# Mixer output projections: low parts of the first three weight tiles made by VectorE, and the first mixer's third tile prepared earlier

## The chip, the cores and the metric

The kernel runs on one core of a Trainium2 chip. The metric is the device time of one execution in microseconds (us); lower is better. Five engines work on one core side by side, each through its own list of instructions in a fixed order: TensorE (PE; its weight loads are listed as PEld), VectorE (DVE), ScalarE (ACT), GpSimd (POOL) and SyncE (SP), which here only issues DMAs. An instruction waits for semaphores that others raise, and while it waits everything behind it on its engine waits too.

## The reference, cut to what matters

Two groups of tokens, 512 and 256, pass through the same two layers. Each layer is a half SwiGLU block, a mixer, and another half SwiGLU block, with a residual sum around each. The change touches only the last step of the two mixers, the product with `w_out`:

```
def mixer_ab(h, ...):                       # layer 0
    z = h @ w_in
    a_out = u * vmix                        # spatial gating, 512 columns
    b_out = window_gqa(q, k, v, sink)       # windowed attention, 512 columns
    return jnp.concatenate([a_out, b_out], axis=-1) @ w_out

def mixer_c(h, w_qkv, rpb, w_out):          # layer 1
    qkv = h @ w_qkv
    o = neighbourhood_attn(q, k, v, rpb)
    return o @ w_out

x = x + mixer(rmsnorm(x, mix_n), ...)
```

All data is float32. `w_out` is 1024 x 1024 in both layers.

## The kernel before, in words

**Tiling.** Activations lie transposed: 8 tiles of 128 features by 768 tokens. A product is cut into output tiles of 128 features (m = 0 to 7) by two halves of 384 tokens (h = 0, 1), and sums over 8 input tiles k. A float32 product is made from three passes on rounded parts: each operand is a high part plus a low part, and `mm3` issues weight-high by data-high, weight-high by data-low, weight-low by data-high. The high part is a ScalarE copy into the rounded type (line 122 for weights, 208 for data), the low part a subtraction source minus high part (line 123 for weights, 209 for data). `wsplit` makes both parts of a weight tile of 128x512; its subtraction runs on GpSimd unless it is given an engine.

**Names in the trace.** `raw` is a weight tile as loaded, `whi` and `wlo` its parts; `o` is the mixer's result before the projection, `oh` and `ol` its parts; `eh` and `el` are parts of two of those tiles made early in the first mixer; `th`, `tl`, `p`, `st` and `tb` belong to the attention; `xold` is the residual, read back from DRAM in the first mixer; `ps_mm` and `ps_aux` are PSUM tiles.

**The projection, `mixer_out`.** Six of the eight input tiles are ready before attention ends; their products come first, for the output tiles m = 0 to 5 (`first`). The last two input tiles follow when attention has ended (`second`). The weights of output tile m come from `rows(m)`. For an even m it loads the weights of two output tiles: one tile of 512 KB with the first four input rows, and one of 256 KB with rows 4 and 5. The second of these is split at once, by ScalarE and VectorE (`unit`); I call it the pair's end tile. Then `rows` splits the four rows of its own m by `wsplit`; I call that m's row tile. So an even m makes two splits and an odd m one.

The first mixer (layer 0) takes the input tiles in the order 4, 5, 0, 1, 2, 3, the second mixer (layer 1) in the order 0, 1, 2, 3, 4, 5. So the first product of an output tile reads the end tile in the first mixer, and the row tile in the second. In the first mixer the output tiles 0 and 1 are begun early, with the two input tiles that are ready first; the splits of the remaining input tiles (`parts`) come between. In the second mixer `ready` splits all six input tiles, both halves, 12 pairs of `oh` and `ol`, before the first product.

**What sets the order.** On TensorE the order is that of the program. Beside the projection, generators that are stepped by a running estimate of TensorE's time put attention in between (`tick`). On all other engines a scheduler orders the instructions as the program is built, by its own estimate of when each could start; that order is fixed when the kernel runs. Loaded weights and `xold` share four buffers (`rawp`), `whi` and `wlo` have five each.

Of the kernel before, what the change touches and what calls it, by code (L numbers as in the profile page):

```python
# [16 lines left out]
P = 128  # L17
# [38 lines left out]
class Trunk:  # L56
# [914 lines left out]
    def mixer_out(self, name, ot, chain, cols=False, begun=None):  # L971

        nc = self.nc
        early, late = (4, 5, 0, 1, 2, 3) if cols else range(KD - 2), (KD - 2, KD - 1)
        oh, ol = ([self.gp.tile([P, T], F32R, tag=f"x{n}{k}", name=f"o{n}{k}") for k in range(KD)] for n in "hl")
        src = (oh, ol)
        self.x = [None] * KD
        old = {}  # L980

        def parts(ks, h):
            c0, c1 = HALVES[h]
            for k in ks:
                self.split(oh[k][:, c0:c1], ol[k][:, c0:c1], ot[k][:, c0:c1])

        def ready(ks, done=()):
            for h in (0, 1):
                parts([k for k in ks if (k, h) not in done], h)
            for k in ks:  # L990
                self.x[k] = self.xp.tile([P, T], F32, tag=f"x{k}", name=f"x{k}")
                if not cols:
                    nc.sync.dma_start(self.x[k], self.xd[k])

        def put(m, h, ps):

            c0, c1 = HALVES[h]
            x = self.x[m]
            if not cols:
                nc.vector.tensor_tensor(out=x[:, c0:c1], in0=ps[:, :H], in1=x[:, c0:c1], op=ALU.add)  # L1000
                return
            if h == 0:
                old[m] = self.rawp.tile([P, T], F32, tag="raw", name="xold")
                nc.sync.dma_start(old[m], self.xd[m])
            for a, b in ((H, TA), (TA, T)) if h else ((0, H),):
                out, rows = self.by_column(x, slice(0, P), a, b)
                nc.vector.tensor_tensor(out=out, in0=rows(ps[:, a - c0 : b - c0]), in1=rows(old[m][:, a:b]), op=ALU.add)

        def plus(m, h, ps):
            x = self.x[m][:, HALVES[h][0] : HALVES[h][1]]  # L1010
            nc.vector.tensor_tensor(out=x, in0=ps[:, :H], in1=x, op=ALU.add)
            self.final(m, *HALVES[h])

        loaded = {}

        def rows(m):
            if m % 2 == 0:
                loaded[4] = self.raw(name, 0, 4, m * P, 2 * P)
                loaded[2] = self.unit(name, 4, 2, m * P, 2 * P)
            c = m % 2 * P  # L1020
            hi, lo = self.wsplit(loaded[4][:, :, c : c + P])
            return [(hi[:, k, :], lo[:, k, :]) for k in range(4)] + [tuple(t[:, c : c + P] for t in k) for k in loaded[2]]

        def first(m, h, w):
            put(m, h, self.proj(w, src, HALVES[h], ks=early))

        def second(m, h):
            st = [tuple(t[:, k, m % 2 * P : m % 2 * P + P] for t in ends[m // 2]) for k in (0, 1)]
            plus(m, h, self.proj([None] * 6 + st, src, HALVES[h], ks=late))

        def end(i):
            if i % 2 == 0:
                loaded["end"] = self.raw(name, KD - 2, 2, i * 2 * P, 4 * P)
            c = i % 2 * 2 * P
            ends.append(self.wsplit(loaded["end"][:, :, c : c + 2 * P]))

        alone = ()
        if begun:
            alone = (0, 1)
            w = [rows(m) for m in alone]  # L1040
            done = [self.proj(w[m], begun, (0, H), ks=early[:2], last=False) for m in alone]
            rest = early[2:]
            with self.tc.high_priority(), self.tc.issue_after(self.exps[-1]):
                parts(rest, 0)
            for m in alone:
                ps = self.proj(w[m], src, HALVES[0], ps=done[m], ks=rest, first=False)
                if m == 0:
                    parts(early, 1)
                    parts(early[:2], 0)
                    ready(early, [(k, h) for k in early for h in (0, 1)])  # L1050
                put(m, 0, ps)
            for m in alone:
                first(m, 1, w[m])
        else:
            ready(early)
        for m in range(len(alone), KD - 2):
            w = rows(m)
            for h in (0, 1):
                first(m, h, w)
        self.drain(chain)  # L1060
        with self.tc.issue_after(self.exps[-1]):
            self.silu()
        ready(late)
        self.ffn_open(self.close("mp"))
        self.ffn_tiles()
        self.mixed = True
        self.norm_begin(self.following)
        ends = []
        w = rows(6)
        end(0)  # L1070
        first(6, 0, w)
        end(1)
        for m in (0, 1):
            second(m, 0)
        first(6, 1, w)
        for m in (2, 3):
            second(m, 0)
        w = rows(7)
        end(2)
        for h in (0, 1):  # L1080
            first(7, h, w)
        end(3)
        for m in range(4, KD):
            second(m, 0)
        self.half_done(0)
        for m in range(KD):
            second(m, 1)
        self.close("xg")
        self.fw = self.open("work", self.other(self.guards["comb"][1]))
        self.half_done(1)  # L1090
# [732 lines left out]
```

## Time and profile before

| | |
|---|---|
| median of 3 runs | 2592.6 us (2591.68 to 2593.29) |
| the profiled execution | 2593.14 us, of which 2591.4 us from first to last instruction |
| TensorE matmul busy | 2552.9 us, 99% |
| VectorE busy | 2234.0 us, 86% |
| ScalarE busy | 1366.5 us, 53% |
| GpSimd busy | 159.4 us, 6% |
| granted TensorE clock, mean | 0.996 |
| weight subtractions on GpSimd | 36, 1349 ns each |
| the same on VectorE | 468 from `raw`, 695 ns each |

The profile names each group of instructions by line, engine, operation and tiles. "Idle before" is the time that the engine stood still just ahead of an instruction, with the instruction that ended the wait behind the arrow. In a timeline the columns are start, duration, engine, line and operation, tiles, shapes and count; neighbours of one kind are merged, and the duration is then that of the group. In a table by windows, PEclk is the share of the full clock that TensorE was granted. The first mixer's projection lies at about 682 to 780 us of the span, the second's at about 2006 to 2100 us.

### The profile page before, as it was taken

How to read it: one execution, taken by the hardware profiler on the slowest of the kernel's cores; microseconds unless marked ns; L12 is line 12 of the kernel's file. 1: busy time of each engine (PE TensorE's matmuls, PEld its weight loads, DVE VectorE, ACT ScalarE, POOL GpSimd, SP SyncE). 2: the span in 40 equal slices, each digit the busy share in tenths (PEclk: the TensorE clock that was granted, in tenths of full speed). 3: DMA queues.
4: the chain of work that ended last, by engine and by line, in shares of the span. 5: the costliest groups of instructions: out<-in, count | busy, mean ns of one | idle time of the engine just before them, and what ended most of it. 6: DMA issues, size and time to landing. Idle time of an engine off the chain costs nothing.

```text
span 2591.4 us, 41313 instructions
## 1 busy us (share of the span) xinstructions
PE 2552.9 (99%) x15114; PEld 2488.1 (96%) x15114; DVE 2234.0 (86%) x4659; ACT 1366.5 (53%) x2869; POOL 159.4 (6%) x255
## 2 busy tenths in 40 slices
PE   8999999999999999999999999999999999999998
PEld 8999999988899999999999999998998999999997
DVE  7988898888789989889998889986776699888897
ACT  7544454556656544445655445454455575444543
POOL 1000000000121000000100000001222220000000
PEclk9999999999999999999999999999999999999999
DMA  7523222321144322223442222241211344222222
GB/s 250 166 84 104 72 76 72 129 95 49 46 123 143 114 66 74 74 66 98 134 111 81 67 73 75 66 145 64 64 64 41 106 132 121 82 73 75 71 67 75
DMA packets 93372, 238.68 MB, mean 92 GB/s; under 512 B 21488, under 2 KB 34288, under 8 KB 93168
## 3 DMA queue, kind: packets, MB, share of 16 engines
q1 hardware_dynamic: 85712, 218.96, 26.2%
q0 software_dynamic: 7168, 16.78, 3.1%
q8 instruction: 119, 1.95, 0.3%
q14 instruction: 85, 0.70, 0.1%
q10 hardware_dynamic: 288, 0.29, 0.0%
HBM read 226.56 MB, written 15.07 MB: 93 GB/s over the span
## 4 chain that ended last, share of the span: by engine, by line
PE 68%; DVE 4%; ACT 1%; issue 0%; DMA 0%; DVEq 0%; ACTq 0%
PE ps_mm L152 42%; PE ps_aux L152 25%; PE ps_aux L156 1%; DVE wlo L123 0%; ACT p L1106 0%; DVE tmp L415 0%; DVE p L1116 0%; DMA raw<-in_w 0%; DVE p L1100 0%; DVE tl L209 0%; DVE qk L1580 0%; DVE sg L589 0%; DVE s L737 0%; DVE y L332 0%; DVE v L588 0%
## 5 line engine op out<-in xcount | busy, mean ns | idle before, releaser
L122 ACT CAST whi<-s 128x512 fp32r<-128x512 f32 x496 | 304.8, 621 | 407.1 <-DVE s L737 178.6
L122 ACT CAST whi<-raw 128x512 fp32r<-128x512 f32 x504 | 305.9, 619 | 227.8 <-PE ps_mm L152 90.9
L123 DVE TENSOR_TENSOR wlo<-s,whi 128x512 fp32r<-128x512 f32 x496 | 338.0, 687 | 60.7 <-ACT whi L122 55.6
L123 DVE TENSOR_TENSOR wlo<-raw,whi 128x512 fp32r<-128x512 f32 x468 | 321.1, 695 | 18.9 <-ACT whi L122 15.2
L152 PE MATMUL ps_aux<-dt,whi 128*128 128x384 f32 x864 | 219.4, 335 | 0.0
L152 PE MATMUL ps_mm<-db,whi 128*128 128x384 f32 x864 | 219.3, 335 | 0.0
L152 PEld LDWEIGHTS ps_aux<-dt,whi 128*128 128x128 f32 x864 | 156.1, 188 | 0.0
L152 PEld LDWEIGHTS ps_mm<-db,whi 128*128 128x128 f32 x864 | 156.1, 188 | 0.0
L152 PE MATMUL ps_aux<-dt,wlo 128*128 128x384 f32 x432 | 144.6, 335 | 1.4 <-DVE wlo L123 1.4
L152 PE MATMUL ps_mm<-xh,whi 128*128 128x512 f32 (+1 forms) x416 | 146.0, 351 | 0.0
L152 PE MATMUL ps_mm<-db,wlo 128*128 128x384 f32 x432 | 144.5, 335 | 0.0
L152 PE MATMUL ps_mm<-xl,whi 128*128 128x512 f32 (+1 forms) x416 | 141.1, 339 | 0.0
L152 PE MATMUL ps_mm<-xh,wlo 128*128 128x512 f32 (+1 forms) x416 | 141.1, 339 | 0.0
L737 DVE TENSOR_TENSOR s<-raw,raw 128x512 f32<-128x512 f32 x124 | 84.3, 687 | 21.9 <-DMA raw<-in_w 21.8
L577 DVE TENSOR_TENSOR u<-ps_aux,u 128x384 f32<-128x384 f32 x176 | 97.5, 554 | 4.5 <-PE ps_aux L152 4.3
L152 PE MATMUL ps_aux<-dh,whi 128*128 128x384 f32 x384 | 97.6, 335 | 0.0
L793 DVE TENSOR_TENSOR x<-ps_aux,x 128x384 f32<-128x384 f32 x160 | 85.5, 553 | 13.7 <-PE ps_aux L152 13.6
L1106 ACT ACTIVATE p<-p,st 128x256 f32<-128x256 f32 (+3 forms) x144 | 68.9, 480 | 50.3 <-DVE st L1104 50.1
L793 DVE TENSOR_TENSOR x<-ps_mm,x 128x384 f32<-128x384 f32 x160 | 86.3, 553 | 7.0 <-PE ps_mm L152 6.8
L123 POOL TENSOR_TENSOR wlo<-raw,whi 128x512 fp32r<-128x512 f32 x36 | 48.3, 1349 | 713.2 <-ACT whi L122 705.4
L572 ACT COPY u<-ps_mm 128x384 f32<-128x384 f32 x176 | 83.4, 474 | 16.2 <-PE ps_mm L152 15.9
L107 POOL DMA_DIRECT2D s<-in_w x64 | 46.9, 764 | 714.8 <-PE ps_aux L152 383.9
(516 smaller groups left out, 8187.6 us busy)
## 6 DMA issues: line engine op xcount, KB each, us to landing
raw<-in_w SPq DMA_DIRECT2D x346, 512.0 KB, 3.7
s<-in_w POOLq DMA_DIRECT2D x64, 256.0 KB, 4.6
xdm<-x SPq DMA_DIRECT2D x16, 384.0 KB, 2.4
x<-in_x SPq DMA_DIRECT2D x16, 192.0 KB, 5.6
tok<-in_xt SPq DMA_DIRECT2D x12, 256.0 KB, 6.3
xold<-xdm SPq DMA_DIRECT2D x8, 384.0 KB, 3.2
x<-xdm SPq DMA_DIRECT2D x8, 384.0 KB, 4.5
out_y<-y SPq DMA_DIRECT2D x8, 384.0 KB, 2.5
```

The source lines that it names most:

```text
L107: (eng or self.nc.sync).dma_start(raw, src, **kw)
L122: nc.scalar.copy(hi, src)
L123: (eng or nc.gpsimd).tensor_tensor(out=lo, in0=src, in1=hi.bitcast(F32), op=ALU.subtract)
L152: self.nc.tensor.matmul(out, lhsT=lhsT, rhs=rhs, start=start, stop=stop, **kw)
L156: self.nc.tensor.transpose(out, src, self.ident)
L572: nc.scalar.copy(e[n, out], bank[key, n])
L577: nc.vector.tensor_tensor(out=t, in0=bank[key, n], in1=t, op=ALU.add)
L737: f = lambda o, x, y, op: self.nc.vector.tensor_tensor(out=o, in0=x, in1=y, op=op)
L793: nc.vector.tensor_tensor(out=o, in0=ps, in1=o, op=ALU.add)
L1106: ins = nc.scalar.activation(outs[i], outs[i], AF.Exp, bias=nm[:, i : i + 1], accum_out=sm[:, i : i + 1])
```

## The change

`rows(m)` hands `wsplit` VectorE as its engine for m = 0, 1 and 2, in both mixers, where GpSimd made these three low parts of row tiles before. And in the first mixer `rows(2)`, that is the loads of the pair 2 and 3, the split of its end tile and the split of row tile 2, is now called inside the loop over the first two output tiles, behind the products of m = 0's first half and ahead of the splits of the second half of `o`. The prepared parts wait in the list `w`. The second mixer has no such call; there `w` starts empty, and `rows` is called in the same place as before.

```
-            hi, lo = self.wsplit(loaded[4][:, :, c : c + P])
+            hi, lo = self.wsplit(loaded[4][:, :, c : c + P], self.nc.vector if m < 3 else None)
...
                 ps = self.proj(w[m], src, HALVES[0], ps=done[m], ks=rest, first=False)
                 if m == 0:
+                    w.append(rows(len(alone)))
                     parts(early, 1)
                     parts(early[:2], 0)
                     ready(early, [(k, h) for k in early for h in (0, 1)])
...
         else:
+            w = []
             ready(early)
         for m in range(len(alone), KD - 2):
-            w = rows(m)
+            st = w.pop() if m < len(w) else rows(m)
             for h in (0, 1):
-                first(m, h, w)
+                first(m, h, st)
```

On TensorE the order of instructions stays as it was. On VectorE, in the first mixer, the subtraction for the end tile of the pair 2 and 3 stood behind the residual sums (`x`) of the first two output tiles before:

```order
L1114 RECIPROCAL st<-st 128x4
L1251 TENSOR_TENSOR o_5936<-ps_aux_7774,tb 64x2x64
L1116 TENSOR_SCALAR p<-p,st 128x256 x4
L1251 TENSOR_TENSOR o_5936<-ps_aux_7774,tb 64x2x64
L1251 TENSOR_TENSOR o_5937<-ps_aux_7774,tb 64x2x64 x2
L1007 TENSOR_TENSOR x_7736<-ps_mm_7758,xold 128x4x64
L123 TENSOR_TENSOR wlo_7818<-raw_7815,whi_7817 128x512
L1007 TENSOR_TENSOR x_7737<-ps_mm_7792,xold 128x2x64
```

Now it is `wlo_7723`, and the row tile of m = 2 is `wlo_7727`, which GpSimd made before. Both stand some 30 instructions earlier on VectorE:

```order
L209 TENSOR_TENSOR ol_7600<-o_5933,oh_7592 128x384
L1359 TENSOR_TENSOR o_5933<-o_5933,ug 128x256
L123 TENSOR_TENSOR wlo_7723<-raw_7720,whi_7722 128x512
L209 TENSOR_TENSOR tl<-ps_aux_7652,th 128x512
L209 TENSOR_TENSOR tl<-ps_aux_7661,th 128x512
L209 TENSOR_TENSOR tl<-ps_aux_7670,th 128x512
L123 TENSOR_TENSOR wlo_7727<-raw_7718,whi_7726 128x512
L1102 ISA p,st<-ps_aux_7682,msk,sink 128x256
```

The first subtraction moved ahead of three `tl` of the attention, the second to the place where `ol_7601`, the first `ol` of the second half, stood; that one and its five followers come behind the four scores (`ISA`) now.

In the second mixer VectorE had this order before, at the end of the 12 `ol` (names 22863 to 22868, each for both halves):

```order
L209 TENSOR_TENSOR ol_22867<-o_21346,oh_22859 128x384
L209 TENSOR_TENSOR ol_22868<-o_21923,oh_22860 128x384
L1474 TENSOR_TENSOR o_22217<-ps_aux_22923,tb 64x512
L209 TENSOR_TENSOR tl<-ps_aux_22941,th 128x512
L209 TENSOR_TENSOR tl<-ps_aux_22953,th 128x512
L1000 TENSOR_TENSOR x_22895<-ps_mm_22919,x_22895 128x384
L1000 TENSOR_TENSOR x_22895<-ps_mm_22969,x_22895 128x384
L123 TENSOR_TENSOR wlo_23103<-raw_23100,whi_23102 128x512
```

With the change four weight subtractions follow the last `ol` (m = 0's row tile is `wlo_22916`, m = 1's `wlo_22990`, the pair's end tile `wlo_23103`, m = 2's row tile `wlo_23107`):

```order
L209 TENSOR_TENSOR ol_22867<-o_21346,oh_22859 128x384
L209 TENSOR_TENSOR ol_22868<-o_21923,oh_22860 128x384
L123 TENSOR_TENSOR wlo_22916<-raw_22907,whi_22915 128x512
L123 TENSOR_TENSOR wlo_22990<-raw_22907,whi_22989 128x512
L123 TENSOR_TENSOR wlo_23103<-raw_23100,whi_23102 128x512
L123 TENSOR_TENSOR wlo_23107<-raw_23098,whi_23106 128x512
L1476 TENSOR_TENSOR o_22217<-ps_aux_22923,tb 64x512
L209 TENSOR_TENSOR tl<-ps_aux_22941,th 128x512
```

Three of the four came from GpSimd's list, and the third moved up from behind the first `x`.

On TensorE in the second mixer the first product of the projection reads those parts in its first three matmuls. This is the changed program, with what each waits for:

```order
L152 MATMUL ps_mm_22811<-xl_18929,whi_22574 128x256
L152 MATMUL ps_mm_22811<-xh_18921,wlo_22575 128x256
L152 MATMUL ps_mm_22919<-oh_22855,whi_22915 128x384 [waits Activation_49]
L152 MATMUL ps_mm_22919<-ol_22863,whi_22915 128x384 [waits DVE_49]
L152 MATMUL ps_mm_22919<-oh_22855,wlo_22916 128x384 [waits DVE_49]
L152 MATMUL ps_aux_22923<-th,vt 128x2x128
```

Before, the row of `wlo_22916` read `[waits Pool_49]`; the other rows are as they were.

On SP, in the first mixer, the loads of the pair 2 and 3 (512 and 256 KB) now stand ahead of the first two `xold` loads instead of behind them. The number of loads is unchanged.

More of the change, by code (lines that the diff above doesn't have):

```diff
@@ L1020, in rows @@
             c = m % 2 * P
-            hi, lo = self.wsplit(loaded[4][:, :, c : c + P])
+            hi, lo = self.wsplit(loaded[4][:, :, c : c + P], self.nc.vector if m < 3 else None)
             return [(hi[:, k, :], lo[:, k, :]) for k in range(4)] + [tuple(t[:, c : c + P] for t in k) for k in loaded[2]]
@@ L1047, in mixer_out @@
                 if m == 0:
+                    w.append(rows(len(alone)))
                     parts(early, 1)
@@ L1054, in mixer_out @@
         else:
+            w = []
             ready(early)
         for m in range(len(alone), KD - 2):
-            w = rows(m)
+            st = w.pop() if m < len(w) else rows(m)
             for h in (0, 1):
-                first(m, h, w)
+                first(m, h, st)
         self.drain(chain)
```

## The prediction

> **What bounds the kernel now.** I read the page first, then who waits for whom on TensorE in the two projections, then the timelines of the engines named there.
>
> ```profile
> PE 2552.9 (99%) x15114; PEld 2488.1 (96%) x15114; DVE 2234.0 (86%) x4659; ACT 1366.5 (53%) x2869; POOL 159.4 (6%) x255
> ...
> L123 DVE TENSOR_TENSOR wlo<-raw,whi 128x512 fp32r<-128x512 f32 x468 | 321.1, 695 | 18.9 <-ACT whi L122 15.2
> ...
> L123 POOL TENSOR_TENSOR wlo<-raw,whi 128x512 fp32r<-128x512 f32 x36 | 48.3, 1349 | 713.2 <-ACT whi L122 705.4
> ```
>
> TensorE is busy 99% of the span and its work is not changed. So the change can only move the few times when TensorE stands still, or runs at a lower clock. These are the waits on it in the first projection (640 to 800 us), the longest alone, and in the second (1995 to 2110 us), where there is only one.
>
> ```profile
> PE ps_mm L152 <- DVE wlo L123: 1.8, 1, 1.8
> ...
> PE ps_mm L152 <- DVE ol L209: 0.8, 1, 0.8
> ...
> PE ps_mm L152 <- DVE ol L209: 0.9, 1, 0.9
> ```
>
> The 1.8 us wait is the change's target. TensorE's and VectorE's timelines show it:
>
> ```profile
> 699.86 0.34 PE L152 MATMUL ps_mm<-ol,whi 128*128 128x384 f32 x1
> 701.98 0.44 PE L152 MATMUL ps_mm<-oh,wlo 128*128 128x384 f32 x1 [1.79 <-DVE wlo L123]
> ...
> 686.99 1.89 DVE L209 TENSOR_TENSOR tl<-ps_aux,th 128x512 fp32r<-128x512 f32 x3 [0.54 <-ACT th L208]
> ...
> 697.43 2.15 DVE L1116 TENSOR_SCALAR p<-p,st 128x256 f32<-128x256 f32 x4
> ...
> 700.80 0.61 DVE L1007 TENSOR_TENSOR x<-ps_mm,xold 128x256 f32<-128x256 f32 x1
> 701.25 0.68 DVE L123 TENSOR_TENSOR wlo<-raw,whi 128x512 fp32r<-128x512 f32 x1
> ```
>
> The third tile's end tile is ready to be split, but VectorE comes to it only after attention and residual sums. The table by windows tells what the wait costs beyond itself; its windows are those at whose borders the clock changes, with an earlier wait for comparison.
>
> ```profile
> core 0: us, PE busy (x) PEld busy (x) DVE busy (x) ACT busy (x) POOL busy (x), PEclk, DMA share, GB/s
> ...
> 290.01:293.42 3.41, 1.96 (x11) 1.64 (x10) 3.41 (x7) 1.33 (x3) 0.00 (x0) 1.00 0.00 0
> 293.42:296.83 3.41, 3.41 (x22) 3.41 (x21) 3.39 (x8) 1.80 (x4) 0.00 (x0) 1.00 0.00 0
> ...
> 699.61:703.02 3.41, 1.62 (x11) 1.26 (x10) 3.04 (x7) 0.00 (x0) 0.00 (x0) 1.00 0.17 25
> 703.02:706.43 3.41, 3.41 (x16) 2.98 (x14) 1.38 (x2) 1.17 (x2) 0.00 (x0) 0.50 0.92 329
> 706.43:709.84 3.41, 3.41 (x27) 3.28 (x28) 2.46 (x10) 0.00 (x0) 0.00 (x0) 1.00 0.30 111
> ```
>
> A window in which TensorE worked 1.62 of 3.41 us was followed by one at half clock, which lost 3.41 x 0.5 = 1.7 us; one with 1.96 us of work was not.
>
> **The change, part by part: what it gives.** First, the 1.8 us wait. The end tile's subtraction now stands ahead of three `tl` that run at 686.99, so it is done before 688, and TensorE wants it at about 700. The wait goes; from start to start the two matmuls are 701.98 - 699.86 = 2.12 us apart where 0.17 is usual, so it gives 1.95 us. With it goes the half-clock window, 1.7 us.
>
> Second, what the moved splits push back. They stand ahead of the `ol` of the second half, for which TensorE waits already.
>
> ```profile
> 691.01 0.33 PE L152 MATMUL ps_mm<-ol,whi 128*128 128x384 f32 x1
> ...
> 693.66 0.45 PE L152 MATMUL ps_mm<-ol,whi 128*128 128x384 f32 x1 [0.85 <-DVE ol L209]
> ...
> 688.79 0.55 DVE L209 TENSOR_TENSOR ol<-o,oh 128x384 fp32r<-128x384 f32 x1
> ...
> 690.88 0.55 DVE L209 TENSOR_TENSOR ol<-o,oh 128x384 fp32r<-128x384 f32 x1
> ...
> 691.89 1.25 DVE L1110 TENSOR_TENSOR st<-sink,st 128x4 f32<-128x4 f32 x1
> ...
> 691.52 1.59 POOL L123 TENSOR_TENSOR wlo<-raw,whi 128x512 fp32r<-128x512 f32 x1 [19.32 <-ACT whi L122]
> ...
> 723.60 0.16 DVE L1110 TENSOR_TENSOR st<-sink,st 128x4 f32<-128x4 f32 x1
> ```
>
> A new `wlo` of 0.69 us takes the place at 688.79, and the first `ol` comes behind the scores, at 691.1 instead of 688.79, done at 691.65; TensorE wants it at 691.1: a new wait of 0.6 us. The old wait at 693.66 (1.0 us from start to start) goes, because it came from the `st` of 1.25 us, which takes 0.16 us when GpSimd's subtraction (691.52) does not run beside it, and that one is gone. Gain 0.4 us; if VectorE is slower than I think the loss is at most 0.7 us (one `wlo`), and if the new wait does not come the gain is the whole 1.0.
>
> The Trainium skill, page "SBUF — State Buffer", section "Who interferes with whom", says that a VectorE instruction with two SBUF inputs and a GpSimd instruction that reads SBUF exclude one another for their whole length. The 1.25 us row agrees.
>
> The splits of m = 0 and 1 are costed at nothing: 2 x 0.69 us more for VectorE, against the 1.14 us by which GpSimd's pair held it up, when a sum took 1.82 us instead of 0.68. The first rows below show that, the others what the next paragraph needs.
>
> ```profile
> 669.25 1.82 DVE L1357 TENSOR_TENSOR o<-o,ug 128x512 f32<-128x512 f32 x1
> ...
> 683.33 0.68 DVE L1357 TENSOR_TENSOR o<-o,ug 128x512 f32<-128x512 f32 x1
> ...
> 663.37 9.19 SPq L107 DMA_DIRECT2D raw<-in_w  x2
> ...
> 701.44 0.88 SPq L1004 DMA_DIRECT2D xold<-xdm  x2
> 702.41 0.86 SPq L107 DMA_DIRECT2D raw<-in_w  x2
> ...
> 710.58 1.14 ACT L122 CAST whi<-raw 128x512 fp32r<-128x512 f32 x2 [5.43 <-DMA raw<-in_w]
> ...
> 714.25 2.18 DVE L1116 TENSOR_SCALAR p<-p,st 128x256 f32<-128x256 f32 x4
> ...
> 718.20 1.04 PE L156 MATMUL ps_aux<-ident,p 128*128 128x128 f32 x8
> ```
>
> The loads moved on SP's queue cost nothing either: the pair's two loads go ahead of the first two `xold`, which then wait for the buffers that come free when m = 1 is split, at about 673 (663.37 + 9.19, where the pair's loads waited in the old order), and their sums stand behind the `ol` of 691 to 694 on VectorE. Next in that queue are `xold` 3 and 4 and the loads of the pair 4 and 5. Those bear on a gain of 4 us: ScalarE waited 5.43 us for them, attention's exponentials stand behind it, and TensorE reads the result (`p`, done at 716.4) at 718.2, later 714.2. In the new order these `xold` wait for the split of m = 3 instead of the sums, so they are issued ahead of 701.44 and compete less with the loads of 702.41. How much that gives no row tells: with nothing gained it costs 716.4 - 714.2 = 2.2 us and a half-clock window, with 2.2 us gained nothing. I take nothing, since the loads had to share the queue with two `xold` issued 1 us ahead of them.
>
> Gain in the first mixer: 1.95 + 1.7 + 0.4 = 4.0 us.
>
> **What it takes.** In the second mixer the first product of m = 0 reads the row tile in its third matmul.
>
> ```profile
> 2004.87 0.63 ACT L122 CAST whi<-raw 128x512 fp32r<-128x512 f32 x1
> ...
> 2005.58 1.28 POOL L123 TENSOR_TENSOR wlo<-raw,whi 128x512 fp32r<-128x512 f32 x1 [3.06 <-ACT whi L122]
> ...
> 2007.33 0.44 PE L152 MATMUL ps_mm<-ol,whi 128*128 128x384 f32 x1 [0.93 <-DVE ol L209]
> 2007.61 0.34 PE L152 MATMUL ps_mm<-oh,wlo 128*128 128x384 f32 x1
> ...
> 2006.52 1.23 DVE L209 TENSOR_TENSOR ol<-o,oh 128x384 fp32r<-128x384 f32 x2
> ...
> 2009.14 4.30 DVE L209 TENSOR_TENSOR ol<-o,oh 128x384 fp32r<-128x384 f32 x9
> 2013.35 0.67 DVE L1474 TENSOR_TENSOR o<-ps_aux,tb 64x512 f32<-64x512 f32 x1
> ```
>
> GpSimd made that low part from 2005.58 to 2006.86, in time for 2007.61. Now it is an instruction of VectorE behind all 12 `ol`, at the place of the row of 2013.35. VectorE gains 0.2 us on the way, since the two `ol` at 2006.52 took 1.23 us beside GpSimd where two of the nine that follow take about 1.03 (0.55 and a pitch of 0.47). So it runs from 2013.15 to 2013.84, and TensorE's third matmul starts at about 2013.9 instead of 2007.61: 6.3 us lost. Behind it on TensorE wait the attention's values and transposes; ScalarE and VectorE wait for these in turn, so nothing of the 6.3 us is made up: TensorE's order is fixed and it had no wait left to give. The bounds are 5.9 (VectorE catches up a little more) and 6.6 us.
>
> A wait of 6.3 us covers at least one whole window of 3.41 us, so a half-clock window follows. What is lost in it depends on where in its windows the wait ends: 0.9 us if late in a window, 1.7 in the middle case, 2.6 if so late that a second window is slowed. I take 1.7. Loss: 6.3 + 1.7 = 8.0 us.
>
> The Trainium skill, page "TensorE: Matmul & The Clock Gate", section "Architectural detail: the array is 16× 32×32, not 1× 128×128", has VectorE's queue as strict first in, first out, which speaks against this part of the change; the program's order gives the same.
>
> **Sum.** 2593.14 (the profiled execution, span 2591.4 and 1.7 around it) - 4.0 + 8.0 = 2597.1 us. The median of the runs is 0.5 below that execution; in one whose windows lie otherwise the old wait falls on a border and costs no half clock, so against the median the gain may be smaller. I leave 2597.1: 0.17% above 2592.6. About 0.2%, or 5.2 us, is what a measurement of this kernel can tell from no change; the border is 2597.8.
>
> **Rivals.** (a) The first mixer's gain is given back. For it: the chain of loads, exponentials and transposes above has 1.8 us of room and TensorE comes 4 us earlier. Against it: the queue is emptier. Price: 2.2 us and a new half-clock window of 1.7 leave 0.1 of the 4.0; 2593.14 + 7.9 = 2601.0, slower. It decides once the loads of pair 4 and 5 land no earlier than before.
>
> (b) The slow window at 703 is not due to the 1.8 us wait and stays. Against it: the rows 290.01 and 699.61. Then the gain is 2.3 and the time 2593.14 - 2.3 + 8.0 = 2598.8, slower.
>
> The Trainium skill, in the page on TensorE named above, section "Why this matters for your kernels", asks only that idle gaps stay under about 3 us, which would make (b) right. The trace speaks against it with 1.62 us of work in the window before the drop.
>
> (c) The second wait does not come, because VectorE has the subtraction done by 2007.6. For it only that it had been so with GpSimd; against it the order. Then the time is 2593.14 - 4.0 = 2589.1, 0.13% faster and still within 0.2%.
>
> **How the numbers follow.** My forecast has a chance of 0.67, with its own range 2595.4 to 2598.6 from the bounds (0.4 us of `ol` to -0.7, 5.9 to 6.6, 0.9 to 2.6, and the old half-clock window there or not); a third of it lies above 2597.8. (a) 0.16, (b) 0.06, (c) 0.11. Slower by over 0.2%: 0.67 x 0.3 + 0.16 + 0.06 = 0.42. Faster: the tail of (c), 0.03. Within 0.2%: 0.55. The range 2594.6 to 2599.4 holds the forecast, (b), and the half of (a) in which only part is given back.
>
> **What would show it.** In the changed profile: no TensorE wait for `wlo` near 700 and clock 1.00 there; a wait of about 0.6 us for `ol` near 691; TensorE some 4 us earlier at the end of the first mixer; in the second a single wait of about 6.3 us for `wlo` of line 123 with the 12 `ol` ahead of it on VectorE, and one half-clock window behind it. I am wrong if that wait is shorter than 5 us, if ScalarE waits as long for the loads at 710 as before and TensorE then waits for `p`, or if other waits appear past 800 us.

## The result, and the profile after

The changed kernel takes 2597.57 us in the median (14 runs, 2595.68 to 2600.12), the kernel before 2591.69 us beside it (14 runs, 2589.86 to 2595.57). The ratio is 1.0018 with a 95% interval of 1.0011 to 1.0025, that is 4.7 us (2.9 to 6.5) slower; the two medians alone lie 5.9 us (0.23%) apart. The interval lies wholly above 1, so the change is slower. By the ratio it stays inside the 0.2% that I called no change, at its upper edge, and the median is 0.5 us from the 2597.1 of the forecast.

From the page of the changed kernel, the busy time of the engines and the weight subtractions on VectorE:

```profile
PE 2552.9 (98%) x15114; PEld 2488.4 (96%) x15114; DVE 2232.3 (86%) x4665; ACT 1367.0 (53%) x2869; POOL 151.3 (6%) x249
...
L123 DVE TENSOR_TENSOR wlo<-raw,whi 128x512 fp32r<-128x512 f32 x474 | 322.7, 690 | 16.0 <-ACT whi L122 12.7
```

TensorE's work is the same 2552.9 us, and six subtractions (474 instead of 468) have come to VectorE. These are the waits on TensorE in the changed kernel, first in the first mixer's projection (640 to 800 us), then in the second's (1990 to 2110 us). Columns: what waits, for whom; us in all, times, the longest.

```profile
PE ps_aux L152 <- DVE tl L209: 1.2, 3, 0.9
PE ps_aux L156 <- ACT whi L122: 0.6, 1, 0.6
PE ps_mm L152 <- DVE ol L209: 0.5, 1, 0.5
...
PE ps_mm L152 <- DVE wlo L123: 6.3, 1, 6.3
PE ps_mm L152 <- DVE ol L209: 0.7, 1, 0.7
```

The 1.8 us wait for `wlo` is no longer among those of the first mixer, and the wait for `ol` is 0.5 instead of 0.8. The second mixer has a new one of 6.3 us. The timeline of TensorE at the two places, then VectorE's:

```profile
690.22 0.44 PE L152 MATMUL ps_mm<-ol,whi 128*128 128x384 f32 x1 [0.46 <-DVE ol L209]
...
2001.12 0.44 PE L152 MATMUL ps_mm<-ol,whi 128*128 128x384 f32 x1 [0.67 <-DVE ol L209]
2007.91 0.69 PE L152 MATMUL ps_mm<-oh,wlo 128*128 128x384 f32 x1 [6.35 <-DVE wlo L123]
```

```profile
685.00 0.68 DVE L123 TENSOR_TENSOR wlo<-raw,whi 128x512 fp32r<-128x512 f32 x1
685.60 1.88 DVE L209 TENSOR_TENSOR tl<-ps_aux,th 128x512 fp32r<-128x512 f32 x3
687.40 0.68 DVE L123 TENSOR_TENSOR wlo<-raw,whi 128x512 fp32r<-128x512 f32 x1
...
689.61 0.55 DVE L209 TENSOR_TENSOR ol<-o,oh 128x384 fp32r<-128x384 f32 x1
...
2002.95 4.30 DVE L209 TENSOR_TENSOR ol<-o,oh 128x384 fp32r<-128x384 f32 x9
2007.17 2.49 DVE L123 TENSOR_TENSOR wlo<-raw,whi 128x512 fp32r<-128x512 f32 x4
```

TensorE could have gone on at 2001.56 and got its low part at 2007.8, when the nine `ol` and the first of four `wlo` were done. The table by windows shows the clock behind that wait:

```profile
1998.92:2002.34 3.42, 1.97 (x14) 1.46 (x12) 3.42 (x9) 3.42 (x10) 0.00 (x0) 1.00 0.00 0
2002.34:2005.75 3.41, 0.00 (x0) 0.00 (x0) 3.41 (x8) 3.41 (x9) 0.00 (x0) 1.00 0.00 0
2005.75:2009.16 3.41, 1.25 (x5) 1.25 (x6) 3.41 (x8) 0.87 (x2) 0.00 (x0) 0.50 0.95 310
2009.16:2012.58 3.42, 3.42 (x15) 3.32 (x14) 1.11 (x2) 0.58 (x1) 0.00 (x0) 0.50 0.98 356
```

Two windows run at half clock (PEclk 0.50, the column behind POOL's). TensorE works in them from 2007.91 to 2012.58, so they cost (2012.58 - 2007.91) x 0.5 = 2.3 us.

Both traces hold the same 15114 matmuls on TensorE in the same order (but for three pairs of neighbours that started almost together), so the start of each can be set against its start before. The distance between the two (after minus before) shows where time comes and goes; the places are named by the time before:

| place (us, before) | after minus before (us) | step (us) |
|---|---|---|
| 30 (start of the program) | -1.4 | -1.4 |
| 640 (ahead of the first mixer's projection) | -1.5 | -0.1 |
| 698 (behind the wait for `ol`) | -1.85 | -0.3 |
| 708 (behind the old wait for `wlo`) | -5.5 | -3.6 |
| 790 (end of that projection) | -5.7 | -0.2 |
| 2004 (ahead of the second projection) | -5.75 | 0 |
| 2012 (behind the new wait for `wlo`, the clock not yet whole) | +2.5 | +8.3 |
| 2560 (near the end) | +2.5 | 0 |

The first mixer gives 4.2 us and the second takes 8.3, net 4.1. The profiled execution of the change (2595.68 us) is the fastest of its 14: it had 1.4 us in hand before any changed instruction ran (the trace before has a half-clock window at 27.2 us that this one lacks), so its span is only 2.4 us longer than before, not 4.1.

### The profile page after: what moved, and what is told of

The parts are those of the page before. It is cut to its first block, busy times and chain, and to the rows that moved or that the text cites. A ratio compares the mean times of both kernels' runs of the same rounds, so it can differ in the third digit from the quotient of the medians.

```text
span 2593.8 us, 41310 instructions
## 1 busy us (share of the span) xinstructions
PE 2552.9 (98%) x15114; PEld 2488.4 (96%) x15114; DVE 2232.3 (86%) x4665; ACT 1367.0 (53%) x2869; POOL 151.3 (6%) x249
## 3 DMA queue, kind: packets, MB, share of 16 engines
q8 instruction: 119, 1.95, 0.3%
## 4 chain that ended last, share of the span: by engine, by line
PE 87%; DVE 8%; ACT 2%; DMA 1%; issue 1%; SPq 0%; DVEq 0%; ACTq 0%
PE ps_mm L152 53%; PE ps_aux L152 33%; DVE wlo L123 1%; PE ps_aux L156 1%; ACT p L1108 1%; DVE p L1102 1%; DMA raw<-in_w 1%; DVE tl L209 0%; DVE tmp L415 0%; DMA x<-in_x 0%; DVE p L1118 0%; ACT whi L122 0%; DVE o L1253 0%; DVE ol L209 0%; DMA first<-in_w 0%
## 5 line engine op out<-in xcount | busy, mean ns | idle before, releaser
L152 PE MATMUL ps_mm<-oh,wlo 128*128 128x384 f32 x252 | 85.1, 338 | 6.3 <-DVE wlo L123 6.3
```

The lines of the kernel that those rows point to most:

```text
L152: self.nc.tensor.matmul(out, lhsT=lhsT, rhs=rhs, start=start, stop=stop, **kw)
```

## Experiments

The kernel before, run on the same chip beside them, had a median of 2593.19 us (27 runs) for the first mixer alone, the second alone, only the early call, and m = 0 ahead; 2592.44 us (33 runs) for the other four. All intervals are 95% intervals of the ratio.

| kernel | median us (runs) | ratio to before | interval |
|---|---|---|---|
| the change | 2597.57 (14) | 1.0018 | 1.0011 to 1.0025 |
| first mixer alone | 2588.49 (11) | 0.9983 | 0.9974 to 0.9992 |
| second mixer alone | 2600.35 (5) | 1.0034 | 1.0022 to 1.0047 |
| first mixer, only the early call | 2588.94 (11) | 0.9987 | 0.9978 to 0.9996 |
| first mixer, only VectorE | 2592.40 (11) | 1.0001 | 0.9992 to 1.0010 |
| first mixer, m = 2 on GpSimd | 2589.04 (11) | 0.9988 | 0.9979 to 0.9997 |
| the change, m = 0 ahead in the second | 2592.10 (11) | 1.0003 | 0.9994 to 1.0012 |
| the change, m = 0 on GpSimd in the second | 2590.29 (11) | 0.9993 | 0.9984 to 1.0002 |
| second alone, m = 0 behind 6 `ol` | 2598.28 (11) | 1.0022 | 1.0012 to 1.0031 |

**The two mixers apart.** First the change in the first mixer alone, as a difference to the changed kernel:

```
-            hi, lo = self.wsplit(loaded[4][:, :, c : c + P], self.nc.vector if m < 3 else None)
+            hi, lo = self.wsplit(loaded[4][:, :, c : c + P], self.nc.vector if cols and m < 3 else None)
```

> The change in the first mixer alone: VectorE makes the low parts of m = 0 to 2 there, and the third tile is prepared early; in the second mixer everything stands as before. My theory: the 1.8 us wait for `wlo` goes, the wait for `ol` is about 0.5 us instead of 0.85, and nothing in the second mixer changes, so 2.1 to 4.0 us faster than before by the median (4.0 where the half-clock window always follows the old wait, 2.1 where it hardly ever does; the medians of the whole change, 5.9 us above before, leave -2.1 if the second mixer costs 8.0). Rival (a), the gain is given back by the loads and the exponentials behind it: within 0.5 us of before. A rival that the whole loss stands elsewhere than in the second mixer: slower than before.

Measured: 0.9983, 4.4 us faster (2.1 to 6.7). This kernel beats the one before and the change. Its profiled execution happens to be the slowest of the 11 (2595.35 us), mostly for reasons ahead of the change. From 560 to 640 us it loses 5.9 us against before: a wait of 1.7 us for an `o` at 594.6 us that took 0.2 us in the changed kernel, and four half-clock windows from 598 to 642 us. In the second mixer it waits 2.1 us on ScalarE's `whi`:

```profile
PE ps_mm L152 <- ACT whi L122: 2.1, 1, 2.1
```

Behind that stands a load: ScalarE's row of the time waits 2.85 us for `raw`.

```profile
2102.48 0.62 ACT L122 CAST whi<-raw 128x512 fp32r<-128x512 f32 x1 [2.85 <-DMA raw<-in_w]
```

In the changed kernel the same instruction waits 1.00 us, and TensorE 0.3. At this place TensorE's wait runs from 0 to 2.4 us over the ten traces, and what sets it is not shown; the step of the change itself, from 640 to 790 us, is -5.6 us here, of which 1.3 lie ahead of 670 us, before the change acts, so 4.3.

Then the second mixer alone, as a difference to the kernel before (with `w` and `st` as in the change):

```
-            hi, lo = self.wsplit(loaded[4][:, :, c : c + P])
+            hi, lo = self.wsplit(loaded[4][:, :, c : c + P], self.nc.vector if not cols and m < 3 else None)
```

> The change in the second mixer alone: VectorE makes the low parts of m = 0 to 2 there; the first mixer stands as before. My theory: one wait of about 6.3 us for `wlo` and 0.9 to 2.6 us of half clock behind it, 8.0 us slower than before (7.2 to 9.2). Rival: the wait itself costs 6.3 us and the half clock is made up, 5.9 to 6.5 us slower. If this and the first mixer alone do not add up to the 5.9 us of the whole change (within 1 us), the two places are not independent, and my sum was right by accident.

Measured: 1.0034, 8.8 us slower (5.7 to 12.2). The two parts add up to -4.4 + 8.8 = 4.4 us by the ratios, and the whole change is 4.7. But the intervals are several us wide, and the medians give -4.7 + 7.2 = 2.5 us against 5.9, so the runs do not settle the test that the expectation set. The traces do better: each place has nearly the same step alone (-4.3 and +8.75 us) as in the whole change (-4.2 and +8.3). As far as they tell, the places are independent. In its trace the step at the wait is +8.75 us (from -0.50 at 2004 to +8.25 at 2012), because here three windows are at half clock behind the 6.4 us wait (the rival's 5.9 to 6.5 us is ruled out by this step, not by the interval of the runs):

```profile
2005.20:2008.61 3.41, 0.94 (x5) 0.42 (x3) 3.41 (x9) 3.41 (x10) 0.00 (x0) 1.00 0.00 0
2008.61:2012.03 3.42, 0.00 (x0) 0.00 (x0) 3.42 (x9) 3.26 (x8) 0.00 (x0) 0.50 0.21 46
2012.03:2015.44 3.41, 2.27 (x8) 2.27 (x9) 2.89 (x6) 0.00 (x0) 0.00 (x0) 0.50 0.99 331
2015.44:2018.86 3.42, 3.42 (x15) 3.32 (x15) 0.68 (x1) 1.07 (x2) 0.00 (x0) 0.50 0.99 372
```

**What in the first mixer gives the gain.** Only the early call, with GpSimd for all row tiles (`None` for the engine in both mixers, as a difference to the changed kernel):

> Only the early preparation of the third tile in the first mixer; GpSimd makes all low parts of row tiles as before, in both mixers. My theory: the end tile is split early by VectorE as in the change, so the 1.8 us wait goes; the first `ol` of the second half keeps its place ahead of the scores, so no 0.5 us wait for it near 690; but GpSimd's subtractions run beside VectorE again (the `st` of 1.25 us or a neighbour) and a wait of 0 to 0.9 us for a later `ol` can stay. So 2.0 to 4.5 us faster than before, within 0.7 us of the first mixer's change alone. Rival: handing the row tiles to VectorE is what gives the gain, and the early call without it leaves more than half of the old wait: at most 1 us faster.

Measured: 0.9987, 3.4 us faster (1.0 to 5.7); the wait near 700 is gone. And only VectorE, without the early call (`cols and m < 3`, and the line `w.append(rows(len(alone)))` taken out):

> In the first mixer VectorE makes the low parts of m = 0 to 2, but the third tile is prepared where it was before; the second mixer as before. My theory: the end tile still stands behind the residual sums, so the wait near 700 stays at 1.5 to 2.2 us, and it is followed by a half-clock window only where it lies in one 3.41 us window almost whole; the wait of 0.85 us for `ol` shrinks to 0 to 0.5. So 0 to 1 us faster than before. Rival: with the row tile of m = 2 on VectorE as well, 0.6 us more stands behind it and the wait grows: 0.5 to 1.5 us slower. If it is 3 us or more faster, the early call was not what gave the gain.

Measured: 1.0001, no difference (2.1 us faster to 2.6 slower). TensorE's wait near 700 is still there:

```profile
PE ps_mm L152 <- DVE wlo L123: 1.9, 1, 1.9
```

The traces show it place by place. These are the steps of the distance to before, as in the table of the result, in us:

| kernel | 680 to 690 (wait for `tl` behind GpSimd's split) | 690 to 694 (waits for `ol`) | 698 to 708 (old wait for `wlo`) |
|---|---|---|---|
| the change | 0.0 | -0.4 | -3.6 |
| first mixer alone | 0.0 | -0.4 | -3.6 |
| first mixer, only the early call | +1.0 | -1.1 | -3.6 |
| first mixer, only VectorE | 0.0 | -1.1 | +0.1 |
| first mixer, m = 2 on GpSimd | +1.0 | -1.1 | -3.6 |

So the early call gives the gain: -3.6 us in all six traces that have it, and none of it where only the engine is changed. That kernel takes only the wait for `ol` away (1.1 us in its trace), and that is too little for these runs to tell.

**The push behind the moved split.** The first mixer's change alone, with m = 2 handed back to GpSimd (`cols and m < 2`):

> As the first mixer's change alone (third tile early, second mixer as before), but GpSimd makes the low part of m = 2 in the first mixer. My theory: the first `ol` of the second half stands ahead of the four scores again, so the 0.46 us wait for it near 690 goes, and nothing else: 0 to 0.5 us faster than the first mixer's change alone, which is 4 to 5 us faster than before. Rival: GpSimd's subtraction beside VectorE's two-input work holds up a later `ol` or sum, and a wait of 0.5 to 1 us comes back: 0.1 to 0.6 us slower than the first mixer's change alone.

Measured: 0.9988, 3.1 us faster than before (0.8 to 5.4), not to be told from the 4.4 of the first mixer alone. The profile settles the mechanism. The wait for `ol` goes, but another takes its place. GpSimd's row, VectorE's and TensorE's:

```profile
684.72 1.27 POOL L123 TENSOR_TENSOR wlo<-raw,whi 128x512 fp32r<-128x512 f32 x1 [570.17 <-ACT whi L122]
```

```profile
684.88 1.53 DVE L209 TENSOR_TENSOR ol<-o,oh 128x384 fp32r<-128x384 f32 x1
686.33 0.41 DVE L1359 TENSOR_TENSOR o<-o,ug 128x256 f32<-128x256 f32 x1
686.66 0.68 DVE L123 TENSOR_TENSOR wlo<-raw,whi 128x512 fp32r<-128x512 f32 x1
687.27 1.87 DVE L209 TENSOR_TENSOR tl<-ps_aux,th 128x512 fp32r<-128x512 f32 x3
```

```profile
688.00 0.38 PE L152 MATMUL ps_aux<-kh,q 64*128 64x256 f32 x1 [0.61 <-DVE tl L209]
```

An `ol` that takes 0.55 us alone takes 1.53 beside GpSimd's subtraction. (The Trainium skill, page "SBUF — State Buffer", section "Who interferes with whom", lets two such instructions exclude one another; these rows agree.) Everything behind it is 1 us late, and TensorE waits 0.61 us for `tl`. By the traces the rival was right: a wait of 0.46 us is exchanged for one of 0.61, and from 680 to 694 us this kernel gains 0.1 us where the first mixer's change alone gains 0.4. The runs cannot tell the two apart.

**How the second wait comes about.** The whole change, with m = 0 prepared ahead of the data's splits in the second mixer:

```
-            w = []
+            w = [rows(0)]
             ready(early)
```

> The whole change, but in the second mixer the weights of m = 0 are prepared ahead of the splits of the data, so that VectorE makes `wlo` of m = 0 before the 12 `ol` instead of behind them. My theory: the 6.3 us wait was only a matter of the place on VectorE's list, so it goes; one more subtraction (0.6 us) stands ahead of the first `ol`, so TensorE's wait for that grows from 0.7 to about 1.3 us. The time is that of the first mixer's change alone plus 0.4 us (0 to 1.0), that is 1.7 to 3.6 us faster than before. Rival: VectorE has no room for three more subtractions in the second mixer wherever they stand, and TensorE waits over 2 us there: no faster than before.

Measured: 1.0003 (1.6 us faster to 3.1 slower), slower than I expected. The 6.3 us wait is gone and the one for `ol` is 1.3 as expected, but there is a third, not foreseen:

```profile
PE ps_mm L152 <- DVE ol L209: 1.3, 1, 1.3
PE ps_mm L152 <- DVE wlo L123: 1.1, 1, 1.1
```

```profile
2010.24 1.27 DVE L209 TENSOR_TENSOR tl<-ps_aux,th 128x512 fp32r<-128x512 f32 x2
2011.44 1.13 DVE L1000 TENSOR_TENSOR x<-ps_mm,x 128x384 f32<-128x384 f32 x2
2012.48 2.09 DVE L123 TENSOR_TENSOR wlo<-raw,whi 128x512 fp32r<-128x512 f32 x3
```

It is m = 1's row tile, behind two `tl` and two sums. From 2004 to 2020 this kernel loses 1.9 us against before (-4.1 to -2.2). By its trace it should be some 2.3 us faster than before (4.2 - 1.9); by the runs it is at most 1.6. The rest stays open. The rival's outcome, no faster than before, is what the runs show, and the two waits come to 2.4 us; but its reason, that VectorE has no room wherever the subtractions stand, does not follow from a trace that loses 1.9 us of 4.2.

Then m = 0 back on GpSimd there, m = 1 and 2 on VectorE (`m < 3 and (cols or m > 0)`):

> The whole change, but in the second mixer GpSimd makes the low part of m = 0 as before; VectorE still makes those of m = 1 and 2 there. My theory: the 6.3 us wait hangs on m = 0 alone and goes with its half clock; the low part of m = 1 stands behind two `tl` and two sums on VectorE, as where m = 0 was put ahead, so TensorE waits about 1.1 us for it. So 4.1 - 1.1 - 0 to 0.4, about 2.5 to 3.0 us faster than before in the profile, and 1 to 2 us slower than the first mixer's change alone. Rival: each of the three low parts costs its share of the 8 us, so this is no faster than before.

Measured: 0.9993, 1.8 us faster (4.1 faster to 0.5 slower), between the first mixer alone and the whole change. Its profiled execution is the slowest of its 11 (2595.19 us); by the steps of its trace (-4.5 us from 670 to 790, +1.4 in the second mixer) it gains 3.1 us, near the 2.5 to 3.0 expected. The waits in the second mixer hold the same 1.1 us for `wlo`, and again one for a load that came late, as in the first mixer's kernel:

```profile
PE ps_mm L152 <- ACT whi L122: 2.4, 1, 2.4
PE ps_mm L152 <- DVE wlo L123: 1.1, 1, 1.1
```

So of the 8.3 us, m = 0 alone makes the long wait, and m = 1 would cost 1.4 us by itself (its step from 2004 to 2020: -1.92 to -0.54). In the changed kernel that cost hides behind the longer wait.

**A shorter wait.** The second mixer alone, with m = 0 between the two halves of the data's splits, as a difference to the second mixer's change alone:

```
-            ready(early)
+            parts(early, 0)
+            w.append(rows(0))
+            ready(early, [(k, 0) for k in early])
```

> The change in the second mixer alone, with the weights of m = 0 prepared between the two halves of the data's splits: VectorE makes its `wlo` behind 6 of the 12 `ol`. My theory: the wait shrinks by six pitches of 0.47 us, from 6.35 to about 3.5 us; the half clock behind it costs 0.9 to 2.6 us, 1.7 in the middle; and m = 1 may wait up to 1.1 us as where m = 0 was put ahead. So 4.0 to 6.0 us slower than before, about 3 to 4 us faster than the second mixer's change alone. Rival: the half clock costs a fixed sum once TensorE stands still over 3 us, or the wait is not set by the `ol` ahead: as slow as the second mixer's change alone. The first mixer stands as before: I also look whether a half-clock window follows its wait near 700; my theory is that this depends on where in the 3.41 us windows the wait lies.

Measured: 1.0022, 5.7 us slower (3.1 to 8.0). TensorE waits 3.53 us, as worked out from six pitches of 0.47:

```profile
2010.59 0.69 PE L152 MATMUL ps_mm<-oh,wlo 128*128 128x384 f32 x1 [3.53 <-DVE wlo L123]
```

In its trace the step is +4.7 us (-0.27 at 2004, +4.43 at 2012), with one half-clock window, so the rival falls; m = 1 shows no wait of its own here. The wait is the length of what stands ahead on VectorE, and the clock comes on top.

**When the clock drops.** Four traces hold the old wait near 700 us: before (shown in the prediction), the kernel with m = 0 between, the one with only VectorE, and the second mixer alone. Their windows, in this order:

```profile
699.47:702.88 3.41, 1.58 (x11) 1.23 (x10) 2.90 (x7) 0.00 (x0) 0.00 (x0) 1.00 0.20 66
702.88:706.29 3.41, 3.41 (x15) 2.97 (x14) 1.38 (x2) 1.17 (x2) 0.00 (x0) 0.50 0.91 299
```

```profile
700.39:703.80 3.41, 1.50 (x10) 1.14 (x8) 3.37 (x8) 0.00 (x0) 0.00 (x0) 1.00 0.16 50
703.80:707.21 3.41, 3.41 (x16) 2.97 (x14) 1.57 (x3) 1.17 (x2) 0.00 (x0) 0.50 0.88 270
```

```profile
697.89:701.31 3.42, 2.46 (x15) 2.13 (x13) 3.35 (x8) 0.00 (x0) 1.01 (x1) 1.00 0.00 0
701.31:704.72 3.41, 2.46 (x17) 2.43 (x18) 1.99 (x5) 0.96 (x2) 0.00 (x0) 1.00 0.59 186
704.72:708.13 3.41, 3.41 (x27) 3.03 (x26) 2.98 (x11) 0.12 (x1) 0.00 (x0) 1.00 0.77 264
```

The wait is 1.8 to 1.9 us each time. Where one window holds it whole (1.5 to 1.6 us of work left), the next is at half clock. In the last trace two windows share it (2.46 us of work in each), and the clock stays at 1.00. So in these traces the same stall costs about 2 us or 3.7, by where it falls.

## Why the prediction came out right

**The 1.8 us wait and its half clock: right.** The prediction had 1.95 + 1.7 = 3.65 us; the step from 698 to 708 is -3.6. No window there is below 1.00:

```profile
696.58:699.99 3.41, 3.41 (x25) 3.38 (x24) 3.34 (x9) 0.42 (x1) 0.45 (x1) 1.00 0.37 115
699.99:703.41 3.42, 3.42 (x27) 3.04 (x26) 2.99 (x10) 0.66 (x2) 0.00 (x0) 1.00 0.75 225
703.41:706.82 3.41, 3.41 (x22) 3.37 (x20) 3.19 (x8) 2.81 (x9) 1.30 (x1) 1.00 0.16 32
```

The remark that against a median the gain may be smaller fits the four traces: one of them has no half-clock window at that wait. The measured 4.4 us (2.1 to 6.7) holds both 2.3 and 4.0, so how often it occurs stays open.

**The wait for `ol`: right.** A new one of 0.6 us was forecast at 691, with 0.4 us won; it is 0.46 at 690.22, and the step by 698 is -0.3 to -0.4.

**The loads of pair 4 and 5: right that they cost nothing.** ScalarE waits 3.36 us for them instead of 5.43, and TensorE's transposes of `p` come at 712.72 without a wait, 5.5 us earlier than before. Rival (a) falls.

```profile
704.01 1.14 ACT L122 CAST whi<-raw 128x512 fp32r<-128x512 f32 x2 [3.36 <-DMA raw<-in_w]
...
712.72 1.04 PE L156 MATMUL ps_aux<-ident,p 128*128 128x128 f32 x8
```

**The splits of m = 0 and 1 on VectorE in the first mixer: right at nothing**, as far as the runs tell: with only VectorE changed the ratio is 1.0001. In that trace and in the changed kernel's, the distance to before moves by less than 0.1 us from 660 to 680 us, where these splits run.

**The second mixer's wait: right.** Forecast 6.3 us with all 12 `ol` ahead; the trace has 6.35, and the second mixer alone is 8.8 us slower by the runs. Rival (c) falls. From start to start the matmul moved by a little less than the 6.3 us forecast: the distance goes from -5.75 to +0.30 us, 6.05, because TensorE starts the matmul just ahead of it 0.46 us sooner (its `ol` is done sooner).

**The half clock behind it: right in kind, the term mis-sized.** The step "I take 1.7" has one half-clock window in its middle case. The change shows two, worth 2.3 us, the second mixer alone three, worth (2018.86 - 2013.17) x 0.5 = 2.8, and only the 3.5 us wait has one. The wait takes most of more than one window: those with 0.00, 0.94 and 1.25 us of work left, and one at half clock with 2.27, are each followed by a slow one. From start to start the slow windows add 2.2 us in the change (+0.30 to +2.51). So the loss is 8.3 us for 8.0 and the gain 4.2 for 4.0; two small errors all but cancel in the net, 4.1 for 4.0.

**Rival (b) falls.** The slow window behind the old wait goes with it, and stays away too when the wait is split: it is there in three of the four traces with the wait, and in none of the six without. The two rows that the prediction set against each other (1.62 and 1.96 us of work) would not have been enough, since in the same trace a window with 2.34 us at 580 us is followed by half clock as well. The Trainium skill, page "TensorE: Matmul & The Clock Gate", section "Why this matters for your kernels", asks for gaps under about 3 us; here gaps of 1.8 to 1.9 us were followed by half clock in three traces of four, so the measurement decides against that bound.

**What the number owes to luck.** The forecast adds its difference of 4.0 us to one execution of 2593.14 us, but the median of the kernel before is 2591.69. The measured difference is 4.7 us by the ratio and 5.9 by the medians. So the 0.5 us between forecast and median hides a base that was 1.4 us too high and a difference 0.7 to 1.9 us too low, and the median stays under the border of 2597.8 by only 0.2 us. The forecast's own range was a choice, too: the bounds named for it add up to 2595.9 to 2601.1 at their ends, not to 2595.4 to 2598.6.

**Not in the prediction:** that m = 1's row tile would be late as well in the second mixer. It changed nothing in the sum, because the wait for m = 0 covers it, and it showed only when that wait was taken away.

## What to carry to other kernels

When a producer is moved to a faster engine, ask first what stands ahead of it in that engine's fixed list: the subtraction fell from 1.28 us to 0.68, and its consumer waited 6.35 us more because all 12 `ol` came first. Change the place where it matters, and only there: the first mixer's change alone is worth 4.4 us (3.4 with nothing but the early call), and the same engine choice carried to the second mixer cost 8.8. Take a long wait away only with an eye on what is late next, since it may cover a second one (1.1 us here).

## What the hardware showed that I had not expected

- In these traces the clock goes by fixed windows of 3.41 us and not by the length of a gap alone. In the trace before, the slow windows of the body start at 27.18, 153.47, 583.55 and 703.02 us, that is 37, 163 and 198 times 3.413 us behind the first. Near 700 us, 1.79 to 1.91 us of idle time in one window brought half clock in the next; the same time in two windows did not. But the busy share is not the whole criterion. Near 700 us windows with 1.58 and 1.62 us of work were followed by half clock. In the first mixer's kernel one with 1.54 was not and one with 2.15 was:

```profile
147.02:150.43 3.41, 1.54 (x9) 1.22 (x8) 1.42 (x3) 0.89 (x2) 0.00 (x0) 1.00 0.00 0
150.43:153.84 3.41, 1.46 (x7) 1.14 (x8) 3.41 (x7) 1.22 (x2) 0.00 (x0) 1.00 0.29 37
153.84:157.26 3.42, 3.42 (x12) 3.42 (x11) 1.92 (x4) 1.97 (x4) 0.00 (x0) 0.50 0.79 235
635.12:638.54 3.42, 2.15 (x16) 2.02 (x17) 3.42 (x9) 1.25 (x2) 0.00 (x0) 1.00 0.00 0
638.54:641.95 3.41, 3.41 (x10) 2.65 (x9) 3.41 (x16) 0.55 (x2) 0.00 (x0) 0.50 0.00 0
```

  Near 580 us a window with 2.3 to 2.7 us of work is followed by half clock in nine of the ten traces, and near 290 us one with about 1.96 us is followed by it in none. What else counts there stays open.
- How large the scatter from such windows and from loads is: one execution of the first mixer's kernel lay 6.9 us above its median, with half-clock windows at 598 to 608 and 639 us and a load that held TensorE up for 2.1 us, none of them near the change. A single profile is no measure of a 4 us change. A step between two traces at the place of the change is a closer one, though it too depends on where the windows lie: the old wait with its clock gave a step of -1.4 us in the second mixer alone, where no slow window followed it, and of 0.0 and +0.1 in the two other kernels that kept it.
